# The first norm's sums of squares: from the feature-major x by VectorE adds and TensorE, or from a second, token-major copy of x by ScalarE's accumulator

## The chip, the cores and the metric

One core of a Trainium2 chip runs the whole kernel. The metric is the device time of one execution in microseconds (us); a smaller one is better. The engines are TensorE (PE in the rows; its weight loads PEld), VectorE (DVE), ScalarE (ACT), GpSimd (POOL) and SyncE (SP), which here only issues DMAs.

## The reference, cut to what matters

Two batches (512 and 256 tokens of width 1024) go through a trunk of two layers with the same weights. The change touches the first norm of the first layer, whose result goes into a projection:

```python
def rmsnorm(x, g, eps=NORM_EPS):
    xf = x.astype(jnp.float32)
    y = xf * lax.rsqrt(jnp.mean(xf * xf, axis=-1, keepdims=True) + eps)
    return (y * g.astype(jnp.float32)).astype(x.dtype)
...
        if layer % 2 == 0:
            h = rmsnorm(x, ln_mix_e[j])
            proj = h @ w_in_e[j]
            qa, ka, va, qb, kb, vb = jnp.split(proj, EVEN_SPLITS, axis=-1)
```

The columns `kb`, `vb` (2 heads each) and `qb` (8 heads) belong to the grouped-query attention, the others to a neighbourhood attention. The q and k heads of the first kind get a norm of their own and a rotary turn. The rest of the trunk (output projection, MLP, a second layer with differential attention) is not touched.

## The kernel before, in words

The 768 tokens of both batches are handled together as NT = 768 columns, in TT = 6 token tiles of 128. x comes transposed from HBM: eight tiles `x0` of 128 features x 768 tokens. The norm's factor (one number for each token) commutes with the projection, so the projection runs on x times the gain alone and the factor is multiplied into its result. Each operand of a matmul is split into a high and a low part (`xh`, `xl` and `whi`, `wlo`), and a product is three matmuls: high x high, high x low, low x high.

**How the start is staged.** `even_attention` first loads, in turn, the eight tiles of x (0.39 MB each) and the first weight group in eight pieces. For each feature tile k it splits the weights and x (L119, L120), and `Norm.add` squares the tile on ACT (L144, L147) and adds the squares up on DVE (L152). `proj_kv` makes the key and value columns: six token tiles `kvp`, 24 matmuls of 128x256 each. Then `proj_q(0)` makes the first four query heads (`qp`, six token tiles of 24 matmuls) and `proj_q(1)` the other four. Each column group has its own weights: two loads of 128x1024, `wtile`, through three buffers `wraw`, four `whi` and four `wlo`.

**Where the factor comes in.** The matmuls `ss` (L161) sum the squares over the 128 partitions for each of the six token tiles, two columns wide, with ones as the moving operand. Then `ms` (DVE, L166) and `rt` (GpSimd's power with exponent -0.5, L167) make the factor. `tables`, which also calls `rstd`, is called from `proj_kv` at its last token tile; `kv_out` can take a `kvp` tile out of PSUM only when `rt` is there. It writes the values `gv`/`gvp` (ACT L419, DVE L420) and runs `norm_rope` on the keys: a square on ACT (L356), then on DVE a reduction (L358), three products (L363, twice L369) and an addition (L372), with a power on GpSimd (L361). The DVE products L369 are the last to read a PSUM tile. A few steps later the result is transposed on TensorE (`qkT`, L388) and split again (L390, L391).

**What orders the work.** PSUM has 8 banks and each PSUM tile takes one: 3 for the tag `mm` and 5 for `at`. Before the change, `kvp` 0 to 2 take the three `mm` banks; `kvp` 3 to 5, `ss` and the first `qp` take the five `at` banks; the second `qp` is again an `mm` tile and needs the bank of `kvp` 0. Every `qkT` is an `at` tile. Each engine runs its instructions in the order in which a scheduler of the framework put them, and so does each DMA queue; almost all loads are on SP's.

Of the kernel before, what the change touches and what calls it, by code (L numbers as in the profile page):

```python
# [11 lines left out]
F32 = mybir.dt.float32  # L12
F32R = mybir.dt.float32r
AF = mybir.ActivationFunctionType
ALU = mybir.AluOpType
AX = mybir.AxisListType

P = 128
D = 1024
KD = D // P  # L20
TS = 512
TP = 256
NT = TS + TP
TT = NT // P
# [13 lines left out]
def kernel(ctx: ExitStack, tc: tile.TileContext, a: dict, y: bass.AP):  # L38
    nc = tc.nc


    cpool = ctx.enter_context(tc.tile_pool(name="cpool", bufs=1))
# [8 lines left out]
    ones = cpool.tile([P, 8], F32, name="ones")  # L51
    nc.vector.memset(ones, 1.0)
    nhalf = cpool.tile([P, 8], F32, name="nhalf")
    nc.scalar.activation(nhalf, ones, AF.Copy, scale=-0.5)
    ones = ones[:, :2]
    gains = cpool.tile([P, 7, KD], F32, name="gains")
    nc.scalar.dma_start(gains[:, :5], a["gains"])
# [3 lines left out]
    def ps_tile(tag, name):  # L61
        return psum.tile([P, 512], F32, tag=tag, name=name, bufs=BANKS[tag])
# [24 lines left out]
    def wtile(src, width):  # L87
        raw, loads = wload(src, width)
        loads[0]()
        hi, lo = whilo(width)  # L90
        wsplit(hi, lo, raw)
        return hi, lo

    def wcol(tiles):


        def col(k, part, c0, w):
            b = (k % 4) * 256 + c0
            return tiles[k // 4][part][:, b : b + w]

        return col

    def wgroup(src):
        return wcol([wtile(src, 1024) for _ in range(2)])
# [27 lines left out]
    class Norm:  # L132
# [22 lines left out]
        def rstd(self, s0=0):  # L155

            n = len(self.tiles)
            ss = ps_tile("at", "ss")
            for i, t in enumerate(self.tiles):
                for j, part in enumerate(self.parts):  # L160
                    nc.tensor.matmul(ss[:, 2 * i : 2 * i + 2], part[:, t * P - s0 : (t + 1) * P - s0], ones,  # L161
                                     start=j == 0, stop=j == len(self.parts) - 1)
            ms = spool.tile([P, TT], F32, tag="ms", name="ms", bufs=2)[:, :n]
            rt = cpool.tile([P, TT], F32, tag="rt", name="rt", bufs=2)[:, :n]
            with tc.high_priority():
                nc.vector.tensor_scalar(ms, ss[:, 0 : 2 * n : 2], 1.0 / D, 1e-6, op0=ALU.mult, op1=ALU.add)  # L166
                nc.gpsimd.tensor_tensor(out=rt, in0=ms, in1=nhalf[:, :n], op=ALU.pow)  # L167
            return rt

# [133 lines left out]
    def xo_tile(name):  # L303
        return xpool.tile([P, NT], F32, tag="xo", name=name, bufs=9)


    def even_attention():
        es = ExitStack()
        ap = es.enter_context(tc.tile_pool(name="eattn", bufs=2))

        xs, loads = [], []
        nm = Norm(lambda: ap.tile([P, NT], F32, tag="v", name="sq", bufs=3))
        raws, x0s = [], []
        for i in range(2):
            raw, ld = wload("w_in_e", 1024, 4)
            raws.append(raw)
            for j in range(4):
                k = 4 * i + j
                x0 = xo_tile("x0")
# [6 lines left out]
        for k in range(KD):  # L326
            c = slice((k % 4) * 256, (k % 4) * 256 + 256)
            wsplit(w0[k // 4][0][:, c], w0[k // 4][1][:, c], raws[k // 4][:, c], k % 2 == 0)
            xs.append(split(x0s[k], "x", gcol(G_E, k)))
        for x0 in x0s:  # L330
            nm.add(x0)
        col0 = wcol(w0)

        ropeE = xo_tile("ropeE").rearrange("p (a t d) -> p a t d", a=2, d=HD)
        nc.scalar.dma_start(ropeE, a["ropeE"])
        qkg = ap.tile([P, 4, HD], F32, tag="qkg", name="qkg", bufs=1)
        nc.scalar.dma_start(qkg, a["qkg"])
        rts, tabs = [], []

        def tables():  # L340
            rts.append(nm.rstd())
            for i, sc in ((0, HD ** -0.5), (1, 1.0)):
                tb = ropeE if i else xo_tile("tabq").rearrange("p (a t d) -> p a t d", a=2, d=HD)
                for j in range(2):
                    nc.vector.scalar_tensor_tensor(
                        out=tb[:, j], in0=ropeE[:, j], scalar=sc,
                        in1=qkg[:, 2 * i + j, None, :].broadcast_to([P, TT, HD]), op0=ALU.mult, op1=ALU.mult)
                tabs.append(tb)
# [41 lines left out]
                nc.scalar.activation(d[:, 0, tk], pt[:, c], AF.Copy)  # L390
                nc.vector.tensor_tensor(out=d[:, 1, tk], in0=pt[:, c], in1=d[:, 0, tk].bitcast(F32), op=ALU.subtract)  # L391

        def qk(name):
            return ap.tile([P, 2, NT], F32R, tag="qk", name=name, bufs=7)


        kT, gv, gq, nv, nqk = [], [], {}, {}, {}

# [23 lines left out]
            norm_rope(ps[:, :P], 2, t, tabs[1], kT)  # L422

        def proj_q(s):
            col = wgroup("w_in_e")
            for j in range(2):
                gq[2 * s + j] = qk(f"gq{2 * s + j}")
            for t in range(TT):
                ps = ps_tile("mm" if s + t else "at", "qp")
                yield from proj_tok(col, xs, t, ps)  # L430
                norm_rope(ps[:, :256], 4, t, tabs[0], [gq[2 * s], gq[2 * s + 1]])

# [176 lines left out]
        x = [None] * KD  # L609
# [547 lines left out]

    hs_ = open_hl()
    o, x, es = even_attention()
    es.close()  # L1160
    hs_, xs, nm, spill = mlp(0, "w_out_e", o, x, hs_)
# [3 lines left out]
    o, x, es = odd_attention(xs, nm, sg, spill)  # L1165
# [18 lines left out]
def _tok(tab):  # L1184

    return np.ascontiguousarray(np.moveaxis(tab.reshape(TT, P, *tab.shape[1:]), 0, 1))
# [27 lines left out]
def _layout(i):  # L1214
    r = np.arange
    pos_s, pos_p = _orders()
    x = np.concatenate([i["x_sample"][0][pos_s], i["x_prompt"][0][pos_p]], 0)
    d = {"xT": np.ascontiguousarray(x.T.reshape(KD, P, NT).transpose(1, 0, 2))}
    g = np.stack([i["ln_mix_e"][0], i["ln_mix_o"][0], i["ln_mlp"][0], i["ln_mlp"][1], i["ln_f"]])
    d["gains"] = np.ascontiguousarray(g.reshape(5, KD, P).transpose(2, 0, 1))  # L1220

# [78 lines left out]
```

## Time and profile before

| | us |
|---|---|
| median of three runs | 1734.74 (1733.23 to 1736.24) |
| the profiled execution, as a run | 1737.35 |
| its span, first to last instruction | 1735.5 |
| PE busy in the span | 1704.4 (98%) |
| DVE / ACT / POOL busy | 1316.8 / 875.5 / 353.1 |

The profiled execution is 2.6 us above the median, and 1.85 us of its time lie outside the span. The table's busy times are sums over the whole span; the change works in the first 60 us, so the stretches and rows of that part are what to read. A matmul's shown duration includes its way through the array: consecutive starts tell its pace.

### The profile page before, as it was taken

To read this page: it belongs to the slowest core of one execution; us is meant where nothing else is said; L and a number is where in the kernel's file an instruction comes from. 1 tells how busy PE (TensorE), PEld (TensorE's weight loads), DVE (VectorE), ACT (ScalarE), POOL (GpSimd) and SP (SyncE) were. 2 spreads that over 40 slices of the span, in tenths; PEclk is the share of its full clock that TensorE was granted. 3 is DMA by queue.
4 is the path that set the end of the run, shared out by engine and by line. 5 is a ranking of instruction groups with operands and counts; after the bars stand their busy time and mean duration, and the time that the engine had idled before them with its cause. 6 is when DMAs were issued, how large, how long until landed. Compare 5 with 4: busy or idle time off the path is not lost. (4 is left out here: it accounts for less than half of the span.)

```text
span 1735.5 us, 28286 instructions
## 1 busy us (share of the span) xinstructions
PE 1704.4 (98%) x10964; PEld 1619.8 (93%) x10964; DVE 1316.8 (76%) x2252; ACT 875.5 (50%) x1561; POOL 353.1 (20%) x379
## 2 busy tenths in 40 slices
PE   8999999999999999999999999999999999999997
PEld 8888888899999999999999999988889999999997
DVE  8888647499877687878676776775899776878785
ACT  7765434365544454444435555554555444544442
POOL 2200000024655300000021222220246554000001
PEclk9999999999999999999999999999999999999999
DMA  5111222314555598653410110112145455986521
GB/s 171 37 47 49 69 78 92 130 46 155 169 168 168 202 337 339 213 164 134 132 51 25 50 41 31 55 59 98 37 154 175 166 168 200 323 307 232 190 89 73
DMA packets 74597, 235.42 MB, mean 136 GB/s; under 512 B 7904, under 2 KB 25056, under 8 KB 74464
## 3 DMA queue, kind: packets, MB, share of 16 engines
q1 hardware_dynamic: 52480, 186.93, 32.4%
q0 software_dynamic: 7168, 25.17, 4.1%
q10 hardware_dynamic: 14816, 21.52, 3.4%
q8 instruction: 86, 1.41, 0.3%
q14 instruction: 47, 0.39, 0.1%
HBM read 182.47 MB, written 50.33 MB: 134 GB/s over the span
## 5 line engine op out<-in xcount | busy, mean ns | idle before, releaser
L1060 PE MATMUL dn<-th,whi 128*128 128x384 f32 x1792 | 462.3, 339 | 1.8 <-DVE th L117 1.3
L860 PE MATMUL up<-c,whi 128*128 128x384 f32 x1808 | 461.8, 337 | 0.5 <-ACT whi L80 0.5
L1060 PEld LDWEIGHTS dn<-th,whi 128*128 128x128 f32 x1792 | 326.8, 188 | 2.4 <-DVE th L117 1.6
L860 PEld LDWEIGHTS up<-c,whi 128*128 128x128 f32 x1808 | 327.1, 188 | 1.7 <-ACT whi L80 1.1
L860 PE MATMUL up<-c,wlo 128*128 128x384 f32 x904 | 303.5, 338 | 4.7 <-DVE wlo L81 4.5
L1060 PE MATMUL dn<-th,wlo 128*128 128x384 f32 x896 | 303.2, 338 | 0.0
L80 ACT ACTIVATE whi<-ch 128x1024 fp32r<-128x1024 f32 x88 | 93.3, 1064 | 172.9 <-PE dn L1060 161.3
L860 PEld LDWEIGHTS up<-c,wlo 128*128 128x128 f32 x904 | 169.7, 188 | 7.6 <-DVE wlo L81 7.6
L845 POOL TENSOR_TENSOR s<-wraw 128x512 f32<-128x512 f32 x60 | 86.6, 1448 | 424.2 <-PE npv L601 258.8
L1060 PEld LDWEIGHTS dn<-th,wlo 128*128 128x128 f32 x896 | 168.8, 188 | 0.0
L80 ACT ACTIVATE whi<-wraw 128x1024 fp32r<-128x1024 f32 (+3 forms) x128 | 116.3, 910 | 91.0 <-PE up L860 52.4
L81 DVE TENSOR_TENSOR wlo<-wraw,whi 128x1024 fp32r<-128x1024 f32 (+3 forms) x132 | 144.2, 1092 | 16.9 <-ACT whi L80 16.6
L81 DVE TENSOR_TENSOR wlo<-ch,whi 128x1024 fp32r<-128x1024 f32 x88 | 107.1, 1222 | 54.6 <-ACT whi L80 49.7
L196 PE MATMUL dqk<-whi,xh 128*128 128x256 f32 x384 | 114.7, 299 | 0.0
L80 ACT ACTIVATE whi<-s 128x1024 fp32r<-128x1024 f32 x60 | 63.6, 1061 | 98.6 <-PE up L860 93.4
L167 POOL TENSOR_TENSOR rt<-ms,nhalf 128x6 f32<-128x6 f32 (+1 forms) x6 | 8.9, 1482 | 503.7 <-DVE ms L166 503.7
L196 PE MATMUL dqk<-whi,xl 128*128 128x256 f32 x384 | 107.5, 280 | 0.0
L196 PE MATMUL dqk<-wlo,xh 128*128 128x256 f32 x384 | 107.2, 279 | 0.0
L81 DVE TENSOR_TENSOR wlo<-s,whi 128x1024 fp32r<-128x1024 f32 x60 | 84.5, 1408 | 29.8 <-ACT whi L80 29.8
L117 DVE TENSOR_TENSOR th<-tr,th 128x1536 fp32r<-128x1536 f32 x56 | 98.1, 1752 | 7.6 <-ACT th L116 7.3
L706 ACT ACTIVATE de<-ds,m 128x512 f32<-128x512 f32 (+1 forms) x96 | 58.3, 612 | 80.9 <-DVE m L704 80.9
L868 DVE TENSOR_TENSOR z<-up,z 128x384 f32<-128x384 f32 x180 | 96.4, 549 | 0.9
(235 smaller groups left out, 3761.9 us busy)
## 6 DMA issues: line engine op xcount, KB each, us to landing
wd<-in_w_down_dram SPq DMA_DIRECT2D x84, 512.0 KB, 5.3
tr<-T SPq DMA_DIRECT2D x56, 768.0 KB, 5.5
wraw<-in_w_up_dram SPq DMA_DIRECT2D x64, 512.0 KB, 3.6
T<-t POOLq DMA_DIRECT2D x64, 384.0 KB, 3.1
T<-z ACTq DMA_DIRECT2D x32, 576.0 KB, 3.0
ch<-in_w_down_dram SPq DMA_DIRECT2D x28, 512.0 KB, 5.6
wraw<-in_w_in_o_dram SPq DMA_DIRECT2D x24, 512.0 KB, 3.6
wraw<-in_w_in_e_dram SPq DMA_DIRECT2D x16, 512.0 KB, 3.7
```

Source lines behind the costliest of these rows:

```text
L80: nc.scalar.activation(hi, raw, AF.Copy)
L81: nc.vector.tensor_tensor(out=lo, in0=raw, in1=hi.bitcast(F32), op=ALU.subtract)
L117: nc.vector.tensor_tensor(out=lo, in0=src, in1=hi.bitcast(F32), op=ALU.subtract)
L167: nc.gpsimd.tensor_tensor(out=rt, in0=ms, in1=nhalf[:, :n], op=ALU.pow)
L196: nc.tensor.matmul(ps[:, :256], st[:, tk], col(k, part, 0, 256), start=(k == 0 and i == 0), stop=(k == KD - 1 and i == 2))
L706: nc.scalar.activation(e, s, AF.Exp, bias=m, scale=1.0, accum_out=l2[:, c : c + 1])
L845: nc.gpsimd.tensor_tensor(out=d_, in0=x_, in1=y_, op=ALU.add)
L860: nc.tensor.matmul(ps, part[a_][:, base + k * P : base + (k + 1) * P], t[:, b_], start=start and k + i == 0, stop=stop and k == 3 and i == 2)
L868: nc.vector.tensor_tensor(out=out, in0=x_, in1=y_, op=op)
L1060: nc.tensor.matmul(ps, w[a_][:, c : c + P], th[:, b_, q], start=i + q + a_ + b_ == 0, stop=i == NG - 1 and q == ND - 1 and a_ == 1)
```

## The change

The sums of squares no longer come from the transposed x. The host hands over a second copy of x, `xt`, with the tokens in the partitions (128 x 6 x 1024; 0.52 MB for each of six loads, 3.15 MB in all). Each load goes into a buffer of the attention's tag `qk` (seven buffers, not otherwise in use yet). ACT squares each half row (128x512) and sums it with its accumulator; DVE adds the two half sums; `factor`, split off from `rstd`, makes `ms` and `rt` as before.

Three things come with it. The weights of `proj_q(0)` are loaded and split ahead of the `xt` loads. The second `qp` tile takes an `at` bank instead of an `mm` bank, in the place of `ss`. And GpSimd computes one power on constants at the start (`one8`, used by nothing).

```diff
+    one8 = cpool.tile([P, 8], F32, name="one8")
+    nc.gpsimd.tensor_tensor(out=one8, in0=ones, in1=nhalf, op=ALU.pow)
...
+    def wsplits(loaded):
+        tiles = []
+        for raw, _ in loaded:
+            tiles.append(whilo(1024))
+            wsplit(*tiles[-1], raw)
+        return wcol(tiles)
...
+            return self.factor(ss[:, 0 : 2 * n : 2])
+
+        def factor(self, ss):
...
-                nc.vector.tensor_scalar(ms, ss[:, 0 : 2 * n : 2], 1.0 / D, 1e-6, op0=ALU.mult, op1=ALU.add)
+                nc.vector.tensor_scalar(ms, ss, 1.0 / D, 1e-6, op0=ALU.mult, op1=ALU.add)
...
-        for x0 in x0s:
-            nm.add(x0)
         col0 = wcol(w0)
+
+        colq = [wload("w_in_e", 1024) for _ in range(2)]
+        for _, ld in colq:
+            ld[0]()
+        colq = wsplits(colq)
+        sums = cpool.tile([P, 2, TT], F32, tag="sums", name="sums", bufs=1)
+        for t in range(TT):
+            xt = qk("xt").rearrange("p a t -> p (a t)")[:, :D].bitcast(F32)
+            nc.sync.dma_start(xt, a["xt"][:, t, :])
+            for i in range(2):
+                xi = xt[:, i * 512 : (i + 1) * 512]
+                nc.scalar.activation(xi, xi, AF.Square, accum_out=sums[:, i, t : t + 1])
+        nc.vector.tensor_tensor(out=sums[:, 0], in0=sums[:, 0], in1=sums[:, 1], op=ALU.add)
+        rts.append(nm.factor(sums[:, 0]))
...
         def tables():
-            rts.append(nm.rstd())
...
         def proj_q(s):
-            col = wgroup("w_in_e")
+            col = wgroup("w_in_e") if s else colq
...
-                ps = ps_tile("mm" if s + t else "at", "qp")
+                ps = ps_tile("mm" if s or t > 1 else "at", "qp")
```

The diff also moves instructions on their engines. On ACT, from the last split of x to the first keys, there stood before (the buffer numbers tell tiles apart; `whi_450` and `whi_456` belong to `proj_q(0)`, `whi_759` and `whi_765` to `proj_q(1)`; `work_366`, `380`, `394` are the first three key tiles):

```order
L119 ACTIVATE xh_165<-x0_100,gains_81 128x768
L147 ACTIVATE sq_185<-x0_99 128x768
L80 ACTIVATE whi_450<-wraw_448 128x1024
L147 ACTIVATE sq_188<-x0_100 128x768
L80 ACTIVATE whi_456<-wraw_454 128x1024
L80 ACTIVATE whi_759<-wraw_757 128x1024
L419 ACTIVATE gv_196<-kvp_198,rt_356 128x2x64
...
L419 ACTIVATE gvp_197<-kvp_323,rt_356 128x2x64
L356 ACTIVATE work_366<-kvp_198,rt_356 128x128
L356 ACTIVATE work_380<-kvp_223,rt_356 128x128
L356 ACTIVATE work_394<-kvp_248,rt_356 128x128
L80 ACTIVATE whi_765<-wraw_763 128x1024
```

There stands now (`whi_175` and `whi_179` belong to `proj_q(0)`, `whi_758` and `whi_764` to `proj_q(1)`; `work_377` is the first key tile):

```order
L129 ACTIVATE xh_167<-x0_102,gains_83 128x768
L83 ACTIVATE whi_121<-wraw_98 128x256
L83 ACTIVATE whi_175<-wraw_171 128x1024
L83 ACTIVATE whi_179<-wraw_172 128x1024
L361 ACTIVATE xt_184,sums_183<-xt_184 128x512 x2
...
L361 ACTIVATE xt_204,sums_183<-xt_204 128x512 x2
L83 ACTIVATE whi_758<-wraw_756 128x1024
L446 ACTIVATE gv_218<-kvp_220,rt_210 128x2x64
...
L446 ACTIVATE gvp_219<-kvp_345,rt_210 128x2x64
L83 ACTIVATE whi_764<-wraw_762 128x1024
L386 ACTIVATE work_377<-kvp_220,rt_210 128x128
```

The twelve half squares stand between the weights of `proj_q(0)` and the values, and the second weight tile of `proj_q(1)` stands ahead of the first key square instead of behind the third.

On PE, around the first transpose of a key, there stood before (`qp_548` is the third `qp` tile; 48 matmuls of the first two stand ahead of it):

```order
L196 MATMUL qp_548<-whi_450,xh_129 128x256
L196 MATMUL qp_548<-wlo_451,xh_129 128x256
L196 MATMUL qp_548<-whi_450,xl_130 128x256
L388 MATMUL qkT_555<-ident_72,work_366 128x128
L196 MATMUL qp_548<-whi_450,xh_135 128x256
L196 MATMUL qp_548<-wlo_451,xh_135 128x256
L388 MATMUL qkT_559<-ident_72,work_380 128x128
```

There stands now (`qp_547` is again the third `qp` tile):

```order
L210 MATMUL qp_547<-whi_179,xh_149 128x256
L210 MATMUL qp_547<-wlo_180,xh_149 128x256
L210 MATMUL qp_547<-whi_179,xl_150 128x256
L418 MATMUL qkT_554<-ident_72,work_377 128x128
L210 MATMUL qp_547<-whi_179,xh_155 128x256
L210 MATMUL qp_547<-wlo_180,xh_155 128x256
L210 MATMUL qp_547<-whi_179,xl_156 128x256
```

The first transpose stands behind 63 matmuls of `qp` instead of 54. Up to the first transpose of attention weights (`gpt_ps`) both orders hold the same 210 matmuls of `qp`, 12 of scores and 18 of `qkT`, but for `ss`. From about the 740th row of PE on, in the same stage, the orders of all engines agree again.

## Rows read from the trace of the kernel before

**Rows 1.** The page's first part (busy time of each engine, its share of the span, instructions) and the line of granted clock of its second part (40 slices of the span).

```profile
PE 1704.4 (98%) x10964; PEld 1619.8 (93%) x10964; DVE 1316.8 (76%) x2252; ACT 875.5 (50%) x1561; POOL 353.1 (20%) x379
...
PEclk9999999999999999999999999999999999999999
```

**Rows 2.** Stretches of the start: start:end, length, then busy time (and instructions) of PE, PEld, DVE, ACT and POOL, granted clock of PE, busy share of the DMA engines, GB/s.

```profile
24.82:26.07 1.25, 1.25 (x14) 1.25 (x13) 1.11 (x1) 0.00 (x0) 0.00 (x0) 1.00 0.00 0
26.07:29.17 3.10, 3.10 (x26) 2.89 (x25) 1.30 (x2) 0.38 (x2) 2.19 (x1) 1.00 0.70 176
29.17:31.70 2.53, 0.00 (x0) 0.03 (x1) 1.83 (x10) 2.53 (x9) 0.32 (x1) 1.00 0.60 201
31.70:34.50 2.80, 2.80 (x24) 2.80 (x25) 2.73 (x17) 2.16 (x8) 2.27 (x6) 1.00 0.00 1
47.60:51.67 4.07, 3.76 (x17) 1.78 (x15) 3.82 (x14) 3.06 (x13) 2.87 (x4) 1.00 0.00 0
```

**Rows 3.** PE in order of time, from the end of `kvp` to the wait: start, duration, engine, line, operation, out<-in, shapes, count, and in brackets the idle time before and what ended it.

```profile
24.70 0.28 PE L196 MATMUL kvp<-whi,xl 128*128 128x256 f32 x1
24.82 1.40 PE L161 MATMUL ss<-ones,acc 128*128 128x2 f32 x12
26.07 0.36 PE L196 MATMUL qp<-whi,xh 128*128 128x256 f32 x1
...
28.77 0.28 PE L196 MATMUL qp<-wlo,xh 128*128 128x256 f32 x1
28.89 0.28 PE L196 MATMUL qp<-whi,xl 128*128 128x256 f32 x1
31.70 0.35 PE L196 MATMUL qp<-whi,xh 128*128 128x256 f32 x1 [2.54 <-DVE work L369]
```

**Rows 4.** ACT and DVE from 5 to 28 us, grouped by line: count, busy time and mean, idle time before.

```profile
L147 ACT ACTIVATE sq<-x 128x768 f32<-128x768 f32 x7 | 5.8, 832 | 0.5 <-DVE acc L152 0.5
...
L152 DVE TENSOR_TENSOR acc<-acc,sq 128x768 f32<-128x768 f32 x7 | 6.7, 950 | 0.0
```

**Rows 5.** Stretches by DMA rate (the last column; columns as in Rows 2).

```profile
5.56:10.30 4.74, 4.74 (x21) 4.61 (x22) 4.24 (x8) 4.61 (x7) 0.00 (x0) 1.00 0.98 337
12.00:18.40 6.40, 6.40 (x57) 6.40 (x56) 6.40 (x12) 6.40 (x10) 0.00 (x0) 1.00 0.99 390
12.00:16.00 4.00, 4.00 (x37) 4.00 (x36) 4.00 (x9) 4.00 (x6) 0.00 (x0) 1.00 1.05 406
18.40:20.00 1.60, 1.60 (x16) 1.60 (x16) 1.60 (x3) 1.10 (x2) 0.00 (x0) 1.00 0.41 108
```

**Rows 6.** ACT in order of time in the second layer, where exponentials of 128x512 with the accumulator follow each other.

```profile
900.50 0.69 ACT L706 ACTIVATE de<-ds,m 128x512 f32<-128x512 f32 x1 [1.41 <-DVE m L704]
901.09 0.19 ACT L706 ACTIVATION_READ_ACCUMULATOR de<-ds,m 128x1 f32 x1
901.18 0.68 ACT L706 ACTIVATE de<-ds,m 128x512 f32<-128x512 f32 x1
901.75 0.20 ACT L706 ACTIVATION_READ_ACCUMULATOR de<-ds,m 128x1 f32 x1
901.84 1.05 ACT L80 ACTIVATE whi<-wraw 128x1024 fp32r<-128x1024 f32 x1
902.79 0.38 ACT L659 ACTIVATE d<-dqkT 128x256 fp32r<-128x256 f32 x1
```

**Rows 7.** The factor: DVE and GpSimd in order of time, and the same power of a later norm.

```profile
26.25 0.17 DVE L166 TENSOR_SCALAR ms<-ss 128x6 f32<-128x6 f32 x1 [0.32 <-PE ss L161]
...
26.57 2.19 POOL L167 TENSOR_TENSOR rt<-ms,nhalf 128x6 f32<-128x6 f32 x1 [25.26 <-DVE ms L166]
...
1437.05 1.35 POOL L167 TENSOR_TENSOR rt<-ms,nhalf 128x6 f32<-128x6 f32 x1
```

**Rows 8.** Behind the factor: ACT, then DVE, in order of time.

```profile
28.80 1.14 ACT L419 ACTIVATE gv<-kvp,rt 128x128 fp32r<-128x128 f32 x4 [4.13 <-POOL rt L167]
...
30.31 0.92 ACT L356 ACTIVATE work<-kvp,rt 128x128 f32<-128x128 f32 x3
31.05 1.12 ACT L80 ACTIVATE whi<-wraw 128x1024 fp32r<-128x1024 f32 x1
...
30.74 0.29 DVE L358 TENSOR_REDUCE ss<-work 128x2 f32<-128x128 f32 x1 [0.68 <-ACT work L356]
...
31.21 0.35 DVE L369 TENSOR_TENSOR work<-kvp,ropeE 128x64 f32<-128x64 f32 x2
31.47 0.28 DVE L358 TENSOR_REDUCE ss<-work 128x2 f32<-128x128 f32 x1
...
32.40 0.27 DVE L358 TENSOR_REDUCE ss<-work 128x2 f32<-128x128 f32 x1
...
33.06 0.34 DVE L369 TENSOR_TENSOR work<-kvp,ropeE 128x64 f32<-128x64 f32 x2
```

**Rows 9.** PE in order of time around a change of form.

```profile
35.29 0.27 PE L388 MATMUL qkT<-ident,work 128*128 128x128 f32 x1
35.32 0.37 PE L196 MATMUL qp<-whi,xh 128*128 128x256 f32 x1
35.52 0.28 PE L196 MATMUL qp<-wlo,xh 128*128 128x256 f32 x1
```

**Rows 10.** Two stretches at the turn from up to down projection in the second layer, columns as in Rows 2.

```profile
1492.00:1497.00 5.00, 3.96 (x21) 3.37 (x20) 1.02 (x1) 2.54 (x3) 0.00 (x0) 1.00 0.89 265
1498.30:1501.70 3.40, 3.40 (x12) 3.40 (x11) 3.40 (x4) 1.48 (x1) 0.00 (x0) 0.50 1.00 374
```

More of the change, by code (lines that the diff above doesn't have):

```diff
@@ L162, in rstd @@
                                      start=j == 0, stop=j == len(self.parts) - 1)
+            return self.factor(ss[:, 0 : 2 * n : 2])
+        def factor(self, ss):
+            n = len(self.tiles)
             ms = spool.tile([P, TT], F32, tag="ms", name="ms", bufs=2)[:, :n]
@@ L309, in even_attention, with qk @@
         ap = es.enter_context(tc.tile_pool(name="eattn", bufs=2))
+        rts = []
+        def qk(name):
+            return ap.tile([P, 2, NT], F32R, tag="qk", name=name, bufs=7)
         xs, loads = [], []
-        nm = Norm(lambda: ap.tile([P, NT], F32, tag="v", name="sq", bufs=3))
+        nm = Norm(None)
         raws, x0s = [], []
@@ L337, in even_attention @@
         nc.scalar.dma_start(qkg, a["qkg"])
-        rts, tabs = [], []
+        tabs = []
         def tables():
-            rts.append(nm.rstd())
             for i, sc in ((0, HD ** -0.5), (1, 1.0)):
@@ L391, in put_T @@
                 nc.vector.tensor_tensor(out=d[:, 1, tk], in0=pt[:, c], in1=d[:, 0, tk].bitcast(F32), op=ALU.subtract)
-        def qk(name):
-            return ap.tile([P, 2, NT], F32R, tag="qk", name=name, bufs=7)
         kT, gv, gq, nv, nqk = [], [], {}, {}, {}
@@ L1217, in _layout @@
     x = np.concatenate([i["x_sample"][0][pos_s], i["x_prompt"][0][pos_p]], 0)
-    d = {"xT": np.ascontiguousarray(x.T.reshape(KD, P, NT).transpose(1, 0, 2))}
+    d = {"xT": np.ascontiguousarray(x.T.reshape(KD, P, NT).transpose(1, 0, 2)), "xt": _tok(x)}
     g = np.stack([i["ln_mix_e"][0], i["ln_mix_o"][0], i["ln_mlp"][0], i["ln_mlp"][1], i["ln_f"]])
```

## The prediction

> **What bounds the kernel now.** I read the page's busy times first: PE is busy for 98% of the span at the granted clock's upper level (1.00, 2.4 GHz) in every slice [rows 1]. So a change of some microseconds in the first 60 us is worth what it gives PE there, and what PE gains or loses lasts, unless PE waits later for something else. Then I read PE in order of time through the start. The keys and values (`kvp`) end at 24.82; the twelve records of `ss` take 1.25 us until 26.07; 24 matmuls of `qp` follow at a pace of 0.117; the last starts at 28.89, and the next at 31.70 [rows 2, 3]. That matmul belongs to the second `qp` tile, which wants the PSUM bank of the first `kvp` tile, and DVE's L369 releases it. PE runs dry at 29.01 and waits 2.69 us (2.54 idle in the row, since a matmul's record is longer than its pace). The reason behind it is the factor: the power ends at 28.76, and the values start at 28.80 after ACT has idled 4.13 us for it [rows 7, 8]. These are the two things that the change can give back: 1.25 + 2.69 = 3.94 us, 0.23% of the time. More isn't on this path.
>
> **What is removed.** ACT loses eight squares, DVE seven additions (6.7 us) [rows 4]. Neither is worth anything by itself: from 10 us to 24.82 PE runs at its own pace (37 matmuls in 4.00 us [rows 5]), so these engines feed it in time. PE loses `ss`: **-1.25 us**.
>
> **When the factor comes.** The `xt` loads stand on SP's queue behind the weights of `proj_q(0)`. Today that queue runs dry at about 18.4: the rate falls from 390 GB/s over 12 to 18.4 us to 108 GB/s behind it [rows 5]. So 3.15 MB follow at 18.4 without a gap; their buffers are free. At 390 GB/s they take 8.07 us and the last lands at 26.5. Bounds: 26.1 at the best rate read (406) and 27.8 at the worst (337) [rows 5]. I take 390, the mean of the stretch just ahead.
>
> The trace has no ACT square with the accumulator. The nearest rows are exponentials of 128x512 that use it: 0.68 and 0.66 us from start to start with the read of the accumulator [rows 6]. Twelve of these take 8.0 us from the first landing (18.4 + 1.3 = 19.7), thus until 27.8; behind the last landing two remain, 26.5 + 1.34 = 27.8 as well. ACT and the queue are equally late. Bounds for one half: 0.57, what the exponential alone takes up to the read, and 0.68.
>
> Then come an addition on DVE with its wake-up (0.3, like `ms`: 0.17 and a gap), `ms` to power 0.32, and the power. Its first run took 2.19, one of the same shape later 1.35 [rows 7]. The power on constants stands at the start, where GpSimd is idle, so I take 1.35 and keep 2.19 as the bound. The values then start at 27.8 + 0.3 + 0.32 + 1.35 + 0.03 = **29.8, 1.0 later than today**.
>
> **From the factor to the bank.** Today 2.90 us lie between the first value (28.80) and PE's restart (31.70) [rows 3, 8]. In the new order of ACT the second weight tile of `proj_q(1)` stands ahead of the first key square instead of behind the third. ACT is in order, DVE's reduction waits for that square, and behind the reduction stand the products that release the bank. A split of this size takes 0.95 us of ACT (901.84 to 902.79) [rows 6]. Its weights land 2.6 us behind the last `xt`, at 29.1, before ACT comes to it at 31.3, so it costs its length and no more. The bank comes free at 29.8 + 2.90 + 0.95 = 33.65.
>
> PE has more to do meanwhile: without `ss`, and with the second `qp` tile in an `at` bank, it has 48 matmuls of 0.117 from 24.82, until 30.45. It waits 3.2 us instead of 2.69: **+0.5 us**.
>
> **The next bank.** `qkT` tiles are `at` tiles. Today the first one takes the bank of `ss`, long free. Now all five hold `kvp` 3 to 5 and `qp` 0 and 1, and the first transpose stands 15 matmuls behind the restart, at 33.65 + 1.76 = 35.4. DVE starts the first reduction at 29.8 + 1.94 + 0.95 = 32.7, the later ones 0.73, 0.93 and 0.93 behind each other (30.74, 31.47, 32.40 [rows 8]; the third step is taken like the second), so `kvp` 3 is begun at 35.3, and its last read ends 1.0 later (32.40 to 33.40 [rows 8]). PE waits until 36.4: **+1.0 us**. Below, 0, should the chain run closer than I think. The following transposes find banks of `kvp` 4 and 5 and of earlier transposes in time by the same spacing.
>
> **What is late next.** Today, between 47.60 and 51.67, PE does 17 matmuls and idles 0.31 us [rows 2]; it is at the scores because the low weights of `proj_q(1)` come late from DVE. Now the first of these is split while DVE waits for the factor. I give that **-0.5 us**: at least the 0.31 idle, at most 2.0, all that 17 matmuls at 0.117 would leave free of 4.07. Against it, the new order changes more often between transposes, scores and projections: 145 changes instead of 136 without `ss` in the rows up to where the orders agree. The matmul behind a transpose takes 0.20 instead of 0.117 [rows 9], so 9 x 0.085 = **+0.7 us**. Zero is possible, since a change may hide behind a wait.
>
> **The sum.** -1.25 + 0.5 + 1.0 - 0.5 + 0.7 = +0.45 us. The profiled execution's 1737.35 would become 1737.8. It lies 2.6 above the median, a difference that the change does not touch; on the median of 1734.74 this makes 1735.2. The change gives back `ss` and spends it: the factor that it wants early comes from 3.15 MB that have to be fetched after everything else.
>
> On the rate of that fetch the Trainium skill (DMA: Bandwidth & Descriptors, Specifications) is stricter than the trace: it puts the limit from HBM for one core at about 358 GB/s. Here rows reach 390 and 406 over several microseconds [rows 5], so I let the rows decide. By the page's figure the loads would end an estimated 0.7 us later and the sum would be about 1735.9.
>
> **Rivals.** *The factor in time.* If the halves run at 0.57 and the loads at 406 GB/s, the last one lands at 26.1 and the values start at 26.1 + 1.14 + 2.0 = 29.2: PE's wait is 2.6 (-0.1 against today). If the chain behind also finds its bank (0 instead of 1.0), no switch costs, and the late weights were worth 1.1, the sum is -1.25 - 0.1 - 1.1 = -2.4: 1732.3. For it: DVE has little to do while it waits. Against it: to take the whole wait away, the bank must be free at 30.45, thus the values must start at 26.6, when the last load has only just landed; faster by over 0.2% is out of reach unless the weights were worth all of 2.0. Chance 0.22, a third of it beyond 0.2%.
>
> *The clock falls.* PE waits longer and twice: 3.2 us, then 1.0 after 1.8 us of work. After 2.69 us of waiting today the clock stays at 1.00, with 24 matmuls in the next 2.80 us [rows 2]. But at the turn to the down projection, after 5 us in which PE was busy for 3.96, the granted clock reads 0.50 (1.2 GHz) for 3.4 us, in which 12 matmuls are done [rows 10]. The point is whether the new wait, with the short one behind it, is more like the second. Then 3.4 us at half pace cost 1.5 to 1.7, on top of +0.45: 1736.8, slower than before. The Trainium skill (TensorE: Matmul & The Clock Gate, What's actually happening) has the clock at the lower level after an idle stretch; rows 2 and 10 agree that it depends on what PE did before. Chance 0.18; with the slow fetch (+1.3) on top it passes 0.2%.
>
> *The power stays slow.* The power on constants does not do what it is there for, since something evicts it or its first cost is another one: 2.19 instead of 1.35, +0.84, 1736.0. Against it: no other instruction of GpSimd stands between the two. Chance 0.1.
>
> **How the numbers follow.** The forecast, 1735.2, takes the remaining 0.5, with its own range from 1734.0 to 1736.6. About 0.2% (3.5 us) is what a measurement of this kernel can tell from no change. Faster by more: a third of 0.22, 0.08. Slower by more: the clock together with the slow fetch, and unseen stalls in the new order, 0.1. Within: 0.82. The range goes from the quick case, 1732.0, to 1738.0, the clock with part of the slow fetch; it holds the time 8 times in 10.
>
> **What would show it.** In the new profile: the last `xt` lands at 26.1 to 27.8, twelve halves with a pace near 0.67, the power at 1.35, the values at 29.8, PE's long wait from 30.45 to about 33.7 and a second one near 35.4 ahead of the first transpose, no half clock behind it, and no stay at the scores for want of low weights. I am wrong if the values start before 28.8 (the fetch was quicker), if the wait for the bank is missing or repeats before each transpose, or if the later stages, whose order is the same, do not keep the shift.

## The result, and the profile after

The changed kernel takes 1740.38 us (median of 10 runs, 1738.91 to 1741.43) against 1736.53 for the kernel before (10 runs, 1733.23 to 1737.81): ratio 1.0023, with a 95% interval of 1.0015 to 1.0031. It is 3.9 us slower, and 1740.38 lies above the forecast range of 1732.0 to 1738.0. The profiled execution, the slowest of the ten, took 1741.43, with a span of 1739.7.

The stretches that matter (start:end, length, busy time and instructions of PE, PEld, DVE, ACT and POOL, granted clock, DMA share, GB/s), the first three against [rows 2], the last two in dense stages of the second layer's attention and of the first down projection:

```profile
19.01:21.49 2.48, 0.28 (x4) 0.08 (x2) 0.95 (x3) 1.06 (x1) 0.00 (x0) 1.00 1.04 410
33.46:36.50 3.04, 0.17 (x3) 0.03 (x1) 1.93 (x11) 3.04 (x10) 0.32 (x1) 1.00 0.63 172
37.83:41.24 3.41, 3.12 (x16) 2.86 (x16) 2.87 (x18) 1.96 (x7) 2.73 (x7) 0.50 0.02 5
890.00:1130.00 240.00, 240.00 (x1974) 222.61 (x1974) 168.01 (x465) 128.42 (x372) 56.71 (x107) 1.00 0.14 41
660.00:800.00 140.00, 140.00 (x797) 140.00 (x796) 112.01 (x95) 61.69 (x58) 0.00 (x0) 1.00 0.66 220
```

PE of the kernel after in order of time, against [rows 3] (`L210` is the matmul of the projections, `L84` the low half of a weight, `L399` the DVE products that release a bank, `L418` the transpose):

```profile
19.01 0.28 PE L210 MATMUL kvp<-whi,xh 128*128 128x256 f32 x1
21.49 0.51 PE L210 MATMUL kvp<-wlo,xh 128*128 128x256 f32 x2 [2.20 <-DVE wlo L84]
...
33.34 0.28 PE L210 MATMUL qp<-whi,xl 128*128 128x256 f32 x1
36.50 0.36 PE L210 MATMUL qp<-whi,xh 128*128 128x256 f32 x1 [2.87 <-DVE work L399]
...
38.56 0.41 PE L210 MATMUL qp<-whi,xl 128*128 128x256 f32 x1
39.27 0.45 PE L418 MATMUL qkT<-ident,work 128*128 128x128 f32 x1 [0.29 <-DVE work L399]
```

What released the two longer waits, against [rows 6 to 8], from DVE's, ACT's and GpSimd's rows of the kernel after:

```profile
20.54 0.56 DVE L375 SCALAR_TENSOR_TENSOR tabq<-ropeE,qkg 128x384 f32<-128x384 f32 x1 [3.29 <-DMA ropeE<-in_ropeE_dram]
21.02 0.42 DVE L84 TENSOR_TENSOR wlo<-wraw,whi 128x256 fp32r<-128x256 f32 x1
```

```profile
23.07 0.63 ACT L361 ACTIVATE xt<-xt 128x512 f32<-128x512 f32 x1 [1.88 <-DMA xt<-in_xt_dram]
23.61 0.19 ACT L361 ACTIVATION_READ_ACCUMULATOR xt<-xt 128x1 f32 x1
23.70 0.62 ACT L361 ACTIVATE xt<-xt 128x512 f32<-128x512 f32 x1
...
30.62 0.19 ACT L361 ACTIVATION_READ_ACCUMULATOR xt<-xt 128x1 f32 x1
30.81 1.06 ACT L83 ACTIVATE whi<-wraw 128x1024 fp32r<-128x1024 f32 x1
32.65 1.14 ACT L446 ACTIVATE gv<-kvp,rt 128x128 fp32r<-128x128 f32 x4 [0.77 <-POOL rt L181]
```

```profile
2.77 1.66 POOL L57 TENSOR_TENSOR one<-ones,nhalf 128x8 f32<-128x8 f32 x1 [1.45 <-ACT nhalf L54]
31.29 1.33 POOL L181 TENSOR_TENSOR rt<-ms,nhalf 128x6 f32<-128x6 f32 x1 [26.86 <-DVE ms L180]
```

Read like that, the start seems to explain all of it. PE stands 2.48 us at 19.0, because a table that needs `ropeE` is ahead of the last low weights on DVE. The first half square starts at 23.07 instead of 19.7, so the values start at 32.65 instead of 29.8. PE waits 3.04 us until 36.50, and then the clock falls to its lower level (1.2 GHz) for 3.41 us, in which 16 matmuls are done. That was the theory with which the experiments began, and as an account of the 3.9 us they refuted it.

The line that matters is the fourth: in 240 us in which PE never idles it did 1974 matmuls. The kernel before, whose instructions have the same order there, did 1992:

```profile
890.00:1130.00 240.00, 240.00 (x1992) 222.51 (x1990) 169.00 (x470) 129.13 (x377) 57.49 (x108) 1.00 0.13 41
```

The eighteen matmuls by which it falls short are 2.2 us at 0.12 each, 850 us behind the change. They are not a gap in the record: the trace of the kernel before holds 10964 matmuls, that of the changed kernel 10952, the twelve of `ss` fewer.

### The profile page after: what moved, and what is told of

Its sections match the earlier page's. It is cut to its first block, busy times and chain, and to the rows that moved or that the text cites. A ratio compares the mean times of both kernels' runs of the same rounds, so it can differ in the third digit from the quotient of the medians.

```text
span 1739.7 us, 28268 instructions
## 1 busy us (share of the span) xinstructions
PE 1707.2 (98%) x10952; PEld 1624.0 (93%) x10952; DVE 1312.5 (75%) x2246; ACT 877.8 (50%) x1577; POOL 347.6 (20%) x380
## 5 line engine op out<-in xcount | busy, mean ns | idle before, releaser
L84 DVE TENSOR_TENSOR wlo<-wraw,whi 128x1024 fp32r<-128x1024 f32 (+3 forms) x132 | 144.0, 1091 | 19.1 <-ACT whi L83 18.6
L84 DVE TENSOR_TENSOR wlo<-ch,whi 128x1024 fp32r<-128x1024 f32 x88 | 107.0, 1222 | 54.8 <-ACT whi L83 51.7
L210 PE MATMUL dqk<-whi,xh 128*128 128x256 f32 x384 | 115.3, 300 | 0.0
L84 DVE TENSOR_TENSOR wlo<-s,whi 128x1024 fp32r<-128x1024 f32 x60 | 86.9, 1448 | 32.2 <-ACT whi L83 32.2
L210 PE MATMUL dqk<-whi,xl 128*128 128x256 f32 x384 | 108.3, 282 | 0.0
L210 PE MATMUL dqk<-wlo,xh 128*128 128x256 f32 x384 | 108.0, 281 | 0.0
```

What stands on the lines that cost most here:

```text
L84: nc.vector.tensor_tensor(out=lo, in0=raw, in1=hi.bitcast(F32), op=ALU.subtract)
L210: nc.tensor.matmul(ps[:, :256], st[:, tk], col(k, part, 0, 256), start=(k == 0 and i == 0), stop=(k == KD - 1 and i == 2))
```

## The experiments

Differences in us are those of the medians on the same chip, "+" is slower than the kernel before. The ratios and their intervals are not taken from these two medians and differ from them by up to 0.9 us.

**The table early.** Only the place of two loads:

```diff
-        nc.scalar.dma_start(ropeE, a["ropeE"])
-        nc.scalar.dma_start(qkg, a["qkg"])
+        nc.sync.dma_start(ropeE, a["ropeE"])    # ahead of the weights of proj_q(0)
+        nc.sync.dma_start(qkg, a["qkg"])
```

> The changed kernel, except that the table ropeE is loaded on the queue of SP ahead of the weights of proj_q(0), so that DVE no longer waits for it (3.3 us there, 2.2 us on PE at 19.0 to 21.5 us). Theory (the late factor sets PE's restart): PE runs dry some 2.3 us earlier and waits that much longer for the same bank; +3 to +5 us against the kernel before, like the changed kernel's +3.9. Rival (the wait for the table is what the change costs): +1.4 to +1.9, 2.2 us better than the changed kernel.

Measured: +5.1, ratio 1.0033 (1.0021 to 1.0045), just above the theory's +3 to +5 and far from the rival. The wait at 19 us is gone and the time is no better. The values start at 30.75 here, and PE restarts 3.85 us behind them, as in the changed kernel (32.65 and 36.50), so the factor sets the restart, and the wait for the table was cover for the wait behind it. PE in order of time, with the wait before its restart:

```profile
34.60 0.55 PE L210 MATMUL qp<-whi,xh 128*128 128x256 f32 x1 [3.54 <-DVE work L399]
```

**The wait filled.**

```diff
                 yield from proj_tok(col, xs, t, ps)
+                if s == 0 and t == 1:
+                    for _ in range(26):
+                        nc.tensor.matmul(ps[:, 256:], xs[7][0][:, :P], col(7, 0, 0, 256), start=True, stop=True)
```

> The changed kernel with 26 matmuls more (3.0 us, their results unused) behind the second qp tile, in the stretch in which PE waits for the bank. Theory (the wait makes the clock fall, and the fall costs 1.5 us): the granted clock stays at 1.00 through 35 to 45 us and the time is 1.5 us below the changed kernel, +2.4 against the kernel before. Rival (the fall has another cause, or costs nothing since DVE and ACT are late there anyway): the clock falls or the time stays at +3.9; if the filling is too long it adds a few tenths.

Measured: +5.6, 1.0035 (1.0023 to 1.0048), more than the theory (+2.4) and the rival (+3.9 and a few tenths) had. In the profile the clock stayed at its upper level, and nothing was gained. It doesn't tell the price of the fall, since the filling was too long: in this execution the values were earlier than in the first one (the power at 30.02 instead of 31.29), so by the chain of 3.85 us from the first value to the restart (32.65 to 36.50 above) the bank was free at an estimated 35.2, before the filling ended at 36.1.

**Half of the second copy.**

```diff
-            nc.sync.dma_start(xt, a["xt"][:, t, :])
+            nc.sync.dma_start(xt, a["xt"][:, t, :512])
             for i in range(2):
-                xi = xt[:, i * 512 : (i + 1) * 512]
+                xi = xt[:, i * 256 : (i + 1) * 256]
```

> The changed kernel with only the first 512 of 1024 features of the second copy loaded and squared (it leaves out half of the sum of squares): 1.57 MB instead of 3.15 MB, twelve squares of 128x256. Theory (loads and squares make the factor late, and it sets the restart): the values start 3 to 4 us earlier (28.7 to 29.7), PE waits under 0.5 us, the clock does not fall: -1 to +0.5 us against the kernel before. Rival (the wait for the table and the new order cost the time): +2 to +4.

Measured: +3.4, 1.0018 (1.0010 to 1.0027), the rival's figure and not the theory's. The values started at 27.49, earlier than in the kernel before, and between 28 and 36 us PE was never idle:

```profile
28.00:36.00 8.00, 8.00 (x70) 8.00 (x69) 5.94 (x34) 6.50 (x22) 3.42 (x8) 1.00 0.09 33
```

So with a factor that comes in time, without the wait for the bank and without the fall, most of the loss was still there. PE still idled 1.48 us for the table's sake at 19 us, so by this run alone the rival stands; the table of lags below settles that, since PE is 0.76 us ahead of the kernel before at 179.5 us here. Against the early table, which has the same tiles and values 3.3 us later (30.75), only 1.8 us were gained.

**The first power alone, in the kernel before.**

```diff
+    one8 = cpool.tile([P, 8], F32, name="one8")
+    nc.gpsimd.tensor_tensor(out=one8, in0=ones, in1=nhalf, op=ALU.pow)
```

> The kernel before with the power on constants alone; nothing else moves on any engine. Theory: the factor's power takes 1.35 instead of 2.19 us, the values start 0.84 us earlier and PE's wait of 2.69 shrinks by as much: -0.8 us against the kernel before. Rival (the power has its first cost again, or the bank waits for something else): 0.

Measured: +3.5, 1.0025 (1.0014 to 1.0036); neither -0.8 nor 0 came. This run spoke most clearly against the first theory: every other instruction of every engine stands where it stood, and the loss is of the size of the whole change's. The power did not even get shorter:

```profile
2.78 1.66 POOL L56 TENSOR_TENSOR one<-ones,nhalf 128x8 f32<-128x8 f32 x1 [1.47 <-ACT nhalf L54]
27.28 2.25 POOL L169 TENSOR_TENSOR rt<-ms,nhalf 128x6 f32<-128x6 f32 x1 [22.83 <-DVE ms L168]
```

What this kernel shares with the changed one is a new tile in the first pool. The pools hand out addresses in order, so in the built program all tiles behind it lie 32 bytes higher in each partition. In the changed kernel, with `one8` and `sums`, it is 96 bytes (`whi` begins at byte 35936 instead of 35840); the pool on the right, with `xh`, `xl` and half of the MLP's input, stays. That gave the second theory: the addresses set the pace of the matmuls.

**The change without its tiles, and tiles without the change.**

```diff
-    one8 = cpool.tile([P, 8], F32, name="one8")
-    nc.gpsimd.tensor_tensor(out=one8, in0=ones, in1=nhalf, op=ALU.pow)
+    nc.gpsimd.tensor_tensor(out=ones, in0=ones, in1=nhalf, op=ALU.pow)
...
-        sums = cpool.tile([P, 2, TT], F32, tag="sums", name="sums", bufs=1)
+        sums = nm.acc[:, : 2 * TT].rearrange("p (a t) -> p a t", a=2)
```

> The changed kernel with the same instructions in the same order, but without the two new tiles: the half sums lie in a tile that stands unused at that time, the first power overwrites ones with ones. All tiles behind lie again at the addresses of the kernel before (in the changed kernel they lie 96 bytes higher). Theory now (the shifted addresses slow the matmuls, mean pace 118.9 instead of 117.0 ns for 128x256, summed over the trace 5 to 6 us): paces as in the kernel before, 4 to 6 us below the changed kernel, -2 to +1 us against the kernel before. Rival (the start costs the 3.9 us: late factor and clock): +3 to +4.5.

```diff
+    pad = cpool.tile([P, 24], F32, name="pad")     # in the kernel before
+    nc.gpsimd.memset(pad, 0.0)
```

> The kernel before with one tile of 96 bytes more in the first pool, written once by GpSimd at the start and used by nothing; every other instruction and its order as before, the tiles behind lie 96 bytes higher, as in the changed kernel. Theory (addresses): pace of 128x256 matmuls 118.5 to 119 ns, +3.5 to +6 us. Rival (the pace has another cause, the start costs the time): 0.

Measured: the change without new addresses -0.8, 0.9997 (0.9988 to 1.0006); the kernel before with 96 unused bytes +4.4, 1.0025 (1.0015 to 1.0034). The same stretch in both, first the change without its tiles, then the kernel before with the pad:

```profile
890.00:1130.00 240.00, 240.00 (x1992) 222.55 (x1991) 169.29 (x469) 129.64 (x378) 57.01 (x107) 1.00 0.14 41
```

```profile
890.00:1130.00 240.00, 240.00 (x1974) 222.50 (x1973) 168.07 (x466) 127.95 (x373) 56.52 (x107) 1.00 0.14 41
```

1992 as in the kernel before, 1974 as in the changed one. The addresses, not the instructions, make the difference, and within the measurement they account for all of it.

The traces say the same matmul by matmul. Counted without `ss` and without the filling, PE's matmuls stand in the same order in all kernels from the 915th on (at about 136 us; in the text ahead it was the 740th row). The table gives by how many us the 1201st (at 179.5 us in the kernel before) and the 9201st (at 1420.3) start later than in the kernel before, in one execution of each kernel; three of the kernels follow further down:

```
kernel                                  addresses   1201st   9201st   between
changed kernel                          +96 bytes   +2.50    +7.86    +5.36
  with the table early                  +96         +0.07    +5.35    +5.28
  with the wait filled                  +96         +1.80    +5.86    +4.06
  with half of the second copy          +96         -0.76    +4.07    +4.83
kernel before with 96 unused bytes      +96         +0.49    +4.94    +4.45
kernel before, power with its own tile  +32         +2.00    +5.13    +3.13
kernel before with 64 unused bytes      +64         +0.96    +4.02    +3.06
changed kernel without its tiles        as before   +0.62    +1.26    +0.64
kernel before, power over ones          as before   +0.11    +0.57    +0.46
kernel before, power and early sums     as before   -1.51    -1.82    -0.31
```

Whatever the start did, the kernels of this table with tiles at new addresses lose 3.1 to 5.4 us between the two matmuls, the others less than 0.7. (The times of the runs differ by less than the column of the 9201st, since the profiled execution of the kernel before loses 2 to 4 us more than every other one between 1491 and 1565 us, where its clock falls [rows 10].)

In the medians the start with the second copy is as good as the old one within the measurement. Its profile still shows the late factor:

```profile
20.36 0.63 ACT L360 ACTIVATE xt<-xt 128x512 f32<-128x512 f32 x1 [0.33 <-DMA xt<-in_xt_dram]
...
30.78 1.14 ACT L445 ACTIVATE gv<-kvp,rt 128x128 fp32r<-128x128 f32 x4 [0.83 <-POOL rt L180]
```

**The power over `ones`, and the sums one tile earlier,** both in the kernel before and without new tiles:

```diff
+    nc.gpsimd.tensor_tensor(out=ones, in0=ones, in1=nhalf, op=ALU.pow)
```

> The kernel before with the power on constants written over ones (which stay ones), so that no address changes; in the earlier run with a tile of its own it was 3.5 us slower. Theory (addresses): the factor comes 0.8 us earlier and the paces are those of the kernel before, -0.8 us. Rival (the power itself costs the 3.5 us, for instance since it delays the start): +3.5.

```diff
                 pend.append((t, ps))
+                if t == TT - 2:
+                    rts.append(nm.rstd())     # no longer in tables()
                 if t == TT - 1:
```

> The kernel before with the power on constants over ones, and with the sums ss, the factor's ms and the power called one key tile earlier (behind the fifth kvp tile instead of the sixth). Theory: the values start 2.8 + 0.8 us earlier, so the first banks come free before PE wants them and the wait of 2.69 us goes: -2 to -2.7 us against the kernel before. Rival (the sums of squares come no earlier, since the additions end later, or the next wait takes it): 0 to -0.8.

Measured: the power alone +0.3, 0.9997 (0.9988 to 1.0006), so no cost of it is seen, and its 0.8 us gain is not seen either: the first power of the norm still took 2.25. With the sums earlier too: -2.65, 0.9986 (0.9977 to 0.9994), the theory's figure, but not by the theory's way. The idle time before the restart shrinks from 2.54 [rows 3] to 1.02, but PE now idles 1.94 for the last addition before that:

```profile
24.12 1.47 PE L162 MATMUL ss<-ones,acc 128*128 128x2 f32 x12 [1.94 <-DVE acc L153]
...
31.08 0.36 PE L197 MATMUL qp<-whi,xh 128*128 128x256 f32 x1 [1.02 <-DVE work L369]
```

Together that is more than 2.54, and by 42 us PE has begun 250 matmuls (without `ss`) against 255 in the kernel before. It gets ahead between 48 and 52 us (325 against 317 by 52 us), in the stretch in which the kernel before stays at the scores [rows 2]. The same stretch in the kernel before, with the early sums, and in the change without its tiles:

```profile
48.00:52.00 4.00, 3.79 (x16) 2.03 (x17) 3.75 (x13) 2.66 (x11) 2.89 (x4) 1.00 0.00 0
```

```profile
48.00:52.00 4.00, 3.91 (x27) 2.79 (x26) 4.00 (x10) 2.55 (x11) 2.77 (x4) 1.00 0.33 91
```

```profile
48.00:52.00 4.00, 4.00 (x33) 3.71 (x34) 3.56 (x15) 3.82 (x12) 2.24 (x4) 1.00 0.00 0
```

DVE splits the first low weights of `proj_q(1)` at 50.42, 48.21 and 29.98 in these three:

```profile
50.42 1.21 DVE L81 TENSOR_TENSOR wlo<-wraw,whi 128x1024 fp32r<-128x1024 f32 x1
```

```profile
48.21 1.22 DVE L82 TENSOR_TENSOR wlo<-wraw,whi 128x1024 fp32r<-128x1024 f32 x1
```

```profile
29.98 1.22 DVE L83 TENSOR_TENSOR wlo<-wraw,whi 128x1024 fp32r<-128x1024 f32 x1 [0.64 <-ACT whi L82]
```

That fits the reading that these weights hold PE up there; no run moves them alone, so it is not shown.

**Which addresses.** Consecutive starts of matmuls of one width in the traces (behind 45 us), sorted by where the moving and the stationary tile begin in the built program, gave a rule to try: 64 bytes instead of 96 (`[P, 16]`), and three pads of 32 bytes.

> The kernel before with one unused tile of 64 bytes in the first pool instead of the 96 of the earlier run: the tiles behind it lie 64 bytes higher. In the traces so far a matmul of 384 columns has a mean pace of 173.7 ns where the addresses of its moving and its stationary tile differ by 32 modulo 64, and 175.5 to 176.0 where they agree modulo 64; one of 256 columns 117.0 against 118.6. Theory (what counts is whether the two tiles differ by 32 modulo 64): 64 bytes change no such pair, paces as before, -0.5 to +0.5 us against the kernel before. Rival (any shift slows): +3 to +4.5.

```diff
+    for pool in (cpool, xpool, rpool):     # rpool: a new pool, first on the right
+        pad = pool.tile([P, 8], F32, name="pad")
+        nc.gpsimd.memset(pad, 0.0)
```

> The kernel before with three unused tiles of 32 bytes, one ahead of the weights, one behind them, and one at the right end, so that the weights (hi and lo) lie at 32 modulo 64 and all activations that meet them in a matmul at 0; orders as before. Theory: all 5350 matmuls of 384 columns run at about 173.7 ns (3920 of them ran at 176.0), the 256-column ones stay at 117: 3920 x 2.3 ns = -9 us against the kernel before. Rival (the pace goes by the tile or the place, not by the pair): +4 to -2.

> The same three tiles in the kernel with the early sums and the power over ones (2.65 us faster than the kernel before): the two effects lie in different stages and add up: -11 to -12 us against the kernel before. Rival: the faster matmuls of the projections only wait longer elsewhere: -3 to -9.

Measured: 64 bytes +2.2, 1.0015 (1.0006 to 1.0023); the three pads -4.6, 0.9977 (0.9969 to 0.9986); with the early sums -7.7, 0.9960 (0.9947 to 0.9973). The rule modulo 64 fell with the first of them: 64 bytes should have changed nothing. The three pads lie between their theory (-9) and their rival (+4 to -2), and with the early sums the two gains add up (-4.6 and -2.65 make -7.3). First the 64 bytes, then the three pads:

```profile
890.00:1130.00 240.00, 240.00 (x1966) 222.54 (x1966) 168.18 (x465) 127.29 (x370) 56.81 (x107) 1.00 0.14 41
```

```profile
660.00:800.00 140.00, 140.00 (x809) 140.00 (x809) 116.03 (x101) 63.97 (x61) 0.00 (x0) 1.00 0.66 218
890.00:1130.00 240.00, 240.00 (x1968) 223.20 (x1968) 167.44 (x464) 129.53 (x377) 56.35 (x106) 1.00 0.14 41
```

The kernel before in the first of these stretches, and the second down projection (1520 to 1680), first in the kernel before, then with the three pads:

```profile
660.00:800.00 140.00, 140.00 (x798) 140.00 (x797) 114.66 (x99) 61.64 (x59) 0.00 (x0) 1.00 0.64 217
1520.00:1680.00 160.00, 160.00 (x911) 160.00 (x910) 128.25 (x112) 71.40 (x68) 0.00 (x0) 1.00 0.64 215
```

```profile
1520.00:1680.00 160.00, 160.00 (x925) 160.00 (x924) 129.10 (x113) 72.52 (x70) 0.00 (x0) 1.00 0.65 216
```

The down projection (384 columns) gets faster with the three pads, 809 matmuls in 140 us instead of 797 to 799, and the attention's projections (256 columns) get slower in both, 1966 and 1968 instead of 1992. Sorted by the distance of the moving from the stationary tile modulo 128, the mean pace in ns (with the number of pairs):

```
distance   384 columns                                  256 columns
0          176.0 before (3924), 175.9 after (5361)      118.6 after (2064)
32         173.4 three pads (5349), 173.8 64 B (1420)   117.0 before (1865)
64         175.5 power with a tile (1422)               117.1 power with a tile (1881)
96         173.7 before (1424)                          119.6 64 B (1872), 119.7 three pads (1881)
```

**The best of both rows.**

```diff
+    pad = xpool.tile([P, 8], F32, name="pad")     # behind the weights, with the early sums
+    nc.gpsimd.memset(pad, 0.0)
```

> The kernel with the early sums (2.65 us faster than the kernel before) and one unused tile of 32 bytes behind the weights, so that the weights and the tiles on the right keep their addresses and only the activations on the left move by 32 bytes. From the traces so far the pace goes by the distance of the moving from the stationary tile modulo 128: 384 columns 176.0 at 0, 175.5 at 64, 173.4 to 173.8 at 32 and 96; 256 columns 117.0 at 32, 117.1 at 64, 118.6 at 0, 119.7 at 96. Here all 384-column pairs lie at 32 or 96 and the 256-column ones stay at 32. Theory (the distance sets it): 3920 matmuls x 2.4 ns = -9.4 us besides the early sums, -10 to -12 us against the kernel before, 3 to 4 us better than the three tiles with their 256-column pairs at 96. Rival (the activations or the weights have a good place of their own, or the stages wait for something else by then): 256-column pace at 119 again or no gain over the three tiles, -6 to -8.

Measured: 1726.74 against 1735.40, -8.7, 0.9949 (0.9935 to 0.9963). It is the best of all kernels here and beats both, by less than the -10 to -12 of the theory. The 256 columns kept their pace (1991) and the first down projection got its (810), but the second one (1520 to 1680) did not, 907 against 911 in the kernel before and 925 with the three pads:

```profile
660.00:800.00 140.00, 140.00 (x810) 140.00 (x809) 116.47 (x102) 64.76 (x62) 0.00 (x0) 1.00 0.65 220
890.00:1130.00 240.00, 240.00 (x1991) 222.58 (x1990) 169.16 (x472) 130.20 (x381) 57.68 (x108) 1.00 0.13 41
1520.00:1680.00 160.00, 160.00 (x907) 160.00 (x907) 127.41 (x111) 71.16 (x68) 0.00 (x0) 1.00 0.63 211
```

That execution took 1730.4, the four others 1725.9 to 1726.9, so this may be a matter of the one execution. Its 384-column pairs at distance 32 have a mean of 175.0 ns, against 173.4 and 173.8 in the table, in which they do not stand: either the execution was slow or the distance is not all that counts. What made it is open.

## Why the prediction was wrong

**The step that failed** is the first one: "a change of some microseconds in the first 60 us is worth what it gives PE there, and what PE gains or loses lasts". It took for granted that behind the start both kernels run alike because their order is alike, and so the sum has nothing for the later stages. What the start gains or loses does last: in the traces the changed kernel's lag is 2.6 us at 140 us and 2.5 at 180. But the later stages added a loss of their own, 5.36 us between 179.5 and 1420.3 us, against 0.64 without the new tiles. The prediction's last sentence named a sign of this kind, "if the later stages, whose order is the same, do not keep the shift", but no cause. Two tiles of 32 and 48 bytes, which the diff shows and the prediction gives no price, moved everything behind them.

From the table of distances: 2064 x (118.6 - 117.0) = 3.3 us for 256 columns; 1424 pairs of 384 columns x (175.85 - 173.69) = 3.1; the other 3924 x (175.85 - 176.02) = -0.7. Together 5.7 us; the pad alone cost 4.4, and the step from the changed kernel to the one without its tiles is 1.0023 against 0.9997, 4.5 us. That addresses are the cause is shown; that it is these pairs in just this measure is not: by the same sum the pad of 64 bytes should cost about 5 us (2.2 measured) and the power with a tile 1.5 (3.5 measured; its trace has lost 2.0 by 179.5 us, with a fall of the clock).

**The start.** The forecast for what the change does there was +0.45. Without the new addresses -0.8 was measured, with an interval of -2.1 to +1.0, so the sum is not refuted. That it fits is in part luck, since several of its terms were off and cancel:

- *When the factor comes* failed in size. Expected first half square 19.7, values 29.8; the changed kernel had 23.07 and 32.65, with the same addresses as before 20.36 and 30.78. The pace of a half (0.63 to 0.66), the rate (410 GB/s in the first stretch above) and the chain behind the last square were as forecast; the first landing was late by 0.7 to 3.4 us. Why is open.
- *The table* was missed. "from 10 us to 24.82 PE runs at its own pace ... so these engines feed it in time" held for the order before, not for the new one on DVE. The 2.48 us show no cost of their own in the medians, as the run with the early table says.
- *From the factor to the bank* held: 36.50 - 32.65 = 3.85, which is the forecast 2.90 + 0.95. That the wait came out at 3.04 (forecast 3.2) is luck: PE ran dry at 33.46 instead of 30.45, and the bank came free at 36.50 instead of 33.65, both about 3 us late. *The next bank* cost 0.5 (0.71 between the starts at 38.56 and 39.27, against 0.21 for the matmuls ahead at the lower clock) instead of 1.0.
- *What is late next* was too small. In the traces PE's lag behind the kernel before, counted as in the table of lags though the orders still differ a little here, goes from +3.78 at the 261st matmul (42.7 us in the kernel before) to +2.35 at the 341st (54.7 us) in the changed kernel, from +1.33 to -0.11 with the early table, and from +1.87 to +0.45 without the new tiles: -1.4 each time, where the late low weights had -0.5 and the changes of form +0.7. This gain made good much of what the late factor cost. No run moves either term by itself.
- *The clock falls*, a rival at 0.18, came true in this profile. It does not set the difference: the mean granted clock of the ten runs is 0.9964, and that of the kernel before 0.9965 over the runs beside the first experiments, 0.9961 with those of the second set; and the profile of the change without its tiles has the same fall, at 35.93 us.
- *The factor in time*, at 0.22, did not come: the values were earlier than 28.8 with half of the copy alone.
- *The power stays slow* did not come, for a reason that stays open. The power took 1.33 here as forecast, but the power on constants did not do it: in the kernel before it left 2.25.
- The waits were priced one for one. Half of the copy is 3.59 us ahead of the early table at the 261st matmul and 0.75 at the 341st: its first low weights of `proj_q(1)` are split at 49.62 instead of 30.02, and it stays at the scores. The medians differ by 1.8. So here a later wait took back most of a gain at the start.
- Two readings were off without harm to the sum. The row of 9s in [rows 1] says 90% or more in each slice and not 1.00, and [rows 10] has 0.50 for 3.4 us. And the 2.6 us by which the profiled execution lies above the median seem to be lost there, since every other trace makes up 2 to 4 us on it between 1491 and 1565 us.

## What to carry to other kernels

Where addresses are handed out in order, as here, a change that adds, drops or resizes a tile moves all tiles behind it, and in this kernel, with PE busy for 98% of the span, that alone was worth from +4.4 to -4.6 us, and -6 on top of the early sums. A time that comes out as forecast is no proof of the way there either: the early sums met their -2 to -2.7 through another stretch than the one forecast, which the traces show when the same matmul is looked up in both. Before a difference of a few tenths of a per cent is put down to the instructions, repeat it with the same addresses, and put an unused tile of the same size into the old kernel. The quick sign in a profile is the number of matmuls in a long stretch far from the change in which PE is busy throughout: it should be the same in both, once it is clear that no records are missing.

## What was not expected of the hardware

The pace of a matmul changed with the addresses of its operands alone: 173.4 to 176.0 ns for 384 columns and 117.0 to 119.7 for 256. Sorted by the distance of the two operands the means fall into the groups of the table, with the two widths wanting different distances (both do well at 32), but one run with 175.0 at 32 does not fit. The Trainium skill (SBUF — State Buffer, A bandwidth-pool intuition that's wrong (but worth ruling out)) gives TensorE's weight load a read port of its own, independent of that of the moving operand; by that one would not expect their addresses to matter to each other. The measurement decides that addresses do matter, by 1.5 to 2.3%; no run here shows the mechanism.

The granted clock fell for 3.4 us in the first 50 us in some executions and not in others: with PE's order of the kernel before it fell at 31.94 us in the profile of the power with a tile of its own, and at 33.46 with the three pads, but not in that of the kernel before or of the 96 unused bytes. So a fall seen in one profile says little about the kernel. And GpSimd's power of the same shape took 1.33, 1.57 and 2.25 us as the first of the norms, with a power on constants ahead of it each time (the changed kernel, the early sums, the kernel before).
